# One pool of three PSUM banks for transposes, column sums and probabilities in a hybrid decoder layer

## The chip, the core and the metric

The kernel runs on one core of a Trainium2 chip. The time is device microseconds of one execution; a profiled execution gives the trace from which all rows below come. TensorE (PE) multiplies and transposes and writes its results into PSUM, which has eight banks of 128 x 512 float32 numbers; VectorE (DVE) and ScalarE (ACT) read the banks and work on the results. The engines have one queue of instructions each, and they meet by semaphores.

## What is computed

One layer of a decoder trunk over 512 tokens, 1024 channels, in float32. The parts that matter here:

```
h = rms_norm(x, attn_norm) * (1.0 + scale_a) + shift_a
... = jnp.split(h @ w_in, IN_OFFSETS, axis=-1)
...
o_a = nsa_mixer(q_a, kc, vc, ks, heads(nvs, G), kw, heads(nvw, G), g_nsa)   # 8 heads, 3 branches
...
q_b = (rms_norm(cq, mla_cq_norm) @ w_uq).reshape(B, S, MLA_HEADS, MLA_QK_DIM)
kv_b = (rms_norm(ckv, mla_ckv_norm) @ w_ukv).reshape(...)
...
o_b = mla_mixer(q_b, k_b, v_b)                                              # 8 heads
x = x + gate_a * ((g_a * o_a + g_b * o_b) @ w_o)
...
x = x + gate_f * ((jax.nn.silu(gt) * val) @ w_down)                         # gated MLP with conv
```

Mixer A (NSA) has a compressed, a selected and a window branch per head; with 512 tokens the selected branch is causal attention over all keys, and so is the window branch. Mixer B (MLA) makes its queries, keys and values from two latents, `cq` and `ckv`. Each large product is done as three float32r products of high and low halves.

## The kernel before, in words

The program has four stages, which follow each other with some overlap: the input projections and the compressed keys and values (to about 145 us of the span), the attention of eight head pairs (about 145 to 530 us), the output projection with the second norm (to about 580 us), and the MLP (to the end).

In the attention stage the code of a round `h` stands in this order: `nsa_head(h)`, `mla_kv(h)`, for even `h` `mla_q_pair(h // 2)` (the queries of two MLA heads), `bgate(h)`, for `h = 3` `kv_group(1)`, `q_head(h + 1)`, `comb_a`, `bgate(8 + h)`, `mla_head(h)`, `comb_b`, and, for `h` below 6, a matrix-vector product on DVE with its column sums (`gemv_cols`) or its row (`gate_out`). Round 7 is written out by halves.

An attention head is done in two halves of the queries (`half`), an NSA head in two branches of two halves each, which makes four passes; I call them A and B (queries 0 to 255, the two branches), C and D (queries 256 to 511). A pass does the score matmuls into two banks `psS`, a minimum over the masked scores on DVE (L762), the exponentials on ACT (L767), a scaling by the reciprocal of the sum (L776 on ACT, L778 on DVE), the transposes of the probabilities `Pt` on PE into banks `psT` (L790), their split into high and low halves (`PTh` on ACT, `PTl` on DVE, helper `split`, L83 and L84), and the products with the values into `psO`. Pass C of an NSA head is followed by the compressed branch (`cmp_lane`, L799 to L819).

`mla_kv(h)` makes `kraw` (normed keys, in a buffer of the tag `qn` of which there is one) and transposes it (L406) and the rotary part `krp` (L410). `mla_q_pair` does four products per pair into banks `psG` (`cqTh`), copies them to `qn` (the same single buffer, once per half) and transposes those (L355, L363). `q_head` squares the queries and sums them by matmuls with ones.

The order of the instructions on each engine is not written by hand: a scheduler places them when the program is built, by the order of the code and priorities, and it takes a tile's buffer from its tag's pool when one comes free. In the built program the tiles of one tag get their buffers in the order in which the code asks for them (in the pools of PSUM with one exception before and two after). The banks are such pools: S, T, O, G, and F, with the numbers in `BANKS` (L68). T holds the transposed probabilities (and the transposes and sums of the first stage and of the second norm); F holds the latent transposes (`kraw`, `krp`, `qn`, `a`, `cqn`, `ckvn`, `kn`), the column sums (`sqT`, `acc`), the rows of `gate_out` and a few accumulators.

Of the kernel before, what the change touches and what calls it, by code (L numbers as in the profile page):

```python
# [17 lines left out]
P = 128  # L18
S = 512
# [8 lines left out]
NF = DFF // P  # L28
# [10 lines left out]
def tile_hybrid_layer(  # L39
# [27 lines left out]

    BANKS = {"S": 2, "T": 2, "O": 1, "G": 2, "F": 1}  # L68

    def bank(tag):  # L70
        return ps.tile([P, 512], F32, name="ps" + tag, tag=tag, bufs=BANKS[tag])

# [154 lines left out]
    def kv_group(g, s1=None, s2=None, tag="G"):  # L227
# [20 lines left out]
        def post_k(th, b):  # L248
            if not tabl:
                for src in (rope_c, rope_s):  # L250
                    rope_table(raw_unit(), src)
            s4 = sm.tile([P, 4], F32, name="s4")
            for i in range(4):
                sumsq(b[:, i * HD:(i + 1) * HD], s4[:, i:i + 1])
            r4 = sm.tile([P, 4], F32, name="r4")
            rstd(r4, s4, HD, [P, 4])
            gk = g_k.rearrange("p a d -> p (a d)")[:, None, :].to_broadcast([P, 2, 256])
            a = rope_2x2(b, th, gk, 2, "kg", tabl[0], tabl[1])
            kn = pj.tile([P, 512], F32, name="kn", tag="qg")
            vec.tensor_mul(kn.rearrange("p (a d) -> p a d", a=4), a.rearrange("p (a d) -> p a d", a=4),  # L260
                           r4.unsqueeze(2).to_broadcast([P, 4, HD]))
            tr = bank("F")
            for br in range(2):
                for tt in range(2):
                    pe.transpose(tr[:, (br * 2 + tt) * P:(br * 2 + tt + 1) * P],
                                 kn[:, (tt * 2 + br) * P:(tt * 2 + br + 1) * P], ident)
            for br in range(2):
                cs = slice(th * 256 + 32 * (1 - br), (th + 1) * 256 + 32 * (1 - br))
                split(Kt[br][0][:, cs], Kt[br][1][:, cs], tr[:, br * 256:(br + 1) * 256])
# [13 lines left out]
    def q_head(h):  # L283
        b = bank("G")
# [8 lines left out]
        act.activation(sq, b, AF.Square)  # L293
        sb = bank("F")
        for t in range(NT):
# [17 lines left out]
    def mla_q_pair(p):  # L313
# [6 lines left out]
        for th in range(2):  # L320
            qn = pj.tile([P, 2, 2, HD], F32, name="qn", tag="qn")
            qr = pj.tile([P, 2, 2, RD], F32, name="qr", tag="qr")
            for tt in range(2):
                t = 2 * th + tt
                ts = slice(t * P, (t + 1) * P)
                b = bank("G")
# [24 lines left out]
            cs = slice(th * 256, (th + 1) * 256)  # L351
            tr = bank("F")
            for h in range(2):
                for tt in range(2):
                    pe.transpose(tr[:, (h * 2 + tt) * P:(h * 2 + tt + 1) * P], qn[:, tt, h, :], ident)  # L355
            for h in range(2):
                tv = tr[:, h * 256:(h + 1) * 256]
                act.activation(qnh[h][:, cs], tv, AF.Copy, scale=gcol)
                vec.scalar_tensor_tensor(qnl[h][:, cs], tv, gcol, f(qnh[h][:, cs]), op0=ALU.mult, op1=ALU.subtract)
            tr = bank("F")  # L360
            for h in range(2):
# [12 lines left out]
    def mla_kv(h):  # L374
# [6 lines left out]
        for th in range(2):  # L381
            b = bank("G")
# [8 lines left out]
            for tt in range(2):  # L391
# [11 lines left out]
                          rk.unsqueeze(2).unsqueeze(3).to_broadcast([P, NT, 2, RD]), op=ALU.mult)  # L403
        tr = bank("F")
        for t in range(NT):
            pe.transpose(tr[:, t * P:(t + 1) * P], kraw[:, t, :], ident)  # L406
        split(knh, knl, tr)
        tr = bank("F")
        for t in range(NT):
# [6 lines left out]
    with tc.tile_pool(name="p1", bufs=1) as p1:  # L416
# [9 lines left out]
        tr = bank("T")  # L426
# [76 lines left out]
        bA = [bank("G"), bank("G"), bank("S"), bank("S")]  # L503
        bF = [bank("O"), bank("F"), None]
        wk = {}
# [31 lines left out]
        tr = bank("T")  # L537
# [8 lines left out]
        for t in range(NT):  # L546
            b = bA[t]
# [14 lines left out]
        bB = [bank("G"), bank("G"), bank("S"), bank("S")]  # L562
        bV1 = bank("F")
        W_PRIO[0] = 100
# [11 lines left out]
        for g in range(2):  # L576
            b = bF[g]
# [36 lines left out]
        for src, nk, dst, nm in ((cqn, 3, cqT, "cqT"), (ckvn, 2, ckvT, "ckvT")):  # L614
            for k in range(nk):
                tr = bank("F")
                for t in range(NT):
                    pe.transpose(tr[:, t * P:(t + 1) * P], src[t][:, k * P:(k + 1) * P], ident)
                hh, hl = slot("cq", f"{nm}h{k}", F32R), slot("cq", f"{nm}l{k}", F32R)
                split(hh, hl, tr)  # L620
                dst.append((hh, hl))
# [82 lines left out]
    def gate_out(row, acc, i):  # L704
        b = bank("F")
        ah, al = (pj.tile([P, 512], F32R, name=n, tag=g) for n, g in (("gh", "t1"), ("gl", "t2")))
        split(ah, al, acc)
        mm(b, onesr, ah, True, False)
        mm(b, onesr, al, False, True)
        act.activation(row[:, i * 512:(i + 1) * 512], b, AF.Copy, scale=0.5)  # L710
# [5 lines left out]
    with tc.tile_pool(name="p2", bufs=1) as p2:  # L716
# [141 lines left out]
        def gemv_cols(acc, c0, dst, plus1):  # L858
            bcols = bank("F")
            for i in range(4):  # L860
# [40 lines left out]
        vec.tensor_mul(fA, fA, colB[:, 0:8])  # L901
        Oa, Ob = bank("O"), bank("F")
        mla_kv(7)
# [11 lines left out]
    with tc.tile_pool(name="p3", bufs=1) as p3:  # L915
# [46 lines left out]
        for th in range(2):  # L962
            for nb in range(2):
                cs = slice(nb * 512, (nb + 1) * 512)
                bs = [bank(s) for s in (("G", "G"), ("S", "S"), ("G", "G"), ("O", "F"))[2 * th + nb]]
                for k in range(KD):
# [15 lines left out]
        def ff_load(i, tag=None):  # L982
            FF[i] = [(bank(("OF" if i == 2 else "GS")[hv]), [load_w([(w_up, (hv * NF + i) * P, P)], 4 * u, 4, None, tag) for u in range(2)])
                     for hv in range(2)]
# [45 lines left out]
        for nh in range(2):  # L1030
            bs = [bank(s) for s in (("O", "F", "T", "T") if nh == 0 else ("G", "G", "S", "S"))]
            for k0, kn in [(k, 1) for k in range(NF - 4 * nh)] + [(NF - 4, 4)] * nh:
# [91 lines left out]
```

## Time and profile before

| | |
|---|---|
| median of 3 runs | 933.03 us (933.02 to 934.61) |
| the profiled execution | 934.68 us |
| its span, first to last instruction | 932.5 us |
| PE busy | 900.3 us, 97% |
| DVE busy | 689.5 us, 74% |
| ACT busy | 510.2 us, 55% |
| DMA | 113 MB, 121 GB/s on average |

A busy share is a mean over the stages. Matmuls overlap in PE's pipeline, so that the mean duration of one is longer than the time from one start to the next.

### The profile page before, as it was taken

The page shows a single profiled execution, that of the slowest core. Times are in us where ns is not written, and L with a number is a line of the kernel's source. Part 1 is how long each engine was busy: PE and PEld are TensorE (multiplying, and loading weights), DVE is VectorE, ACT ScalarE, POOL GpSimd, SP SyncE. Part 2 cuts the span into 40 slices and gives each one's busy share as a digit, 9 for nine tenths or more (in the row PEclk, how much of TensorE's full clock was granted, in tenths as well). Part 3 has the DMA queues.
Part 4 walks back from the last instruction along what each step waited for, and adds up shares of the span by engine and source line. Part 5 has one row for each costly group of instructions (what it writes and reads, how often), then busy time and mean ns, then how long its engine had stood idle before and what let it go on. Part 6 is the DMA issues. An engine that isn't in the chain of part 4 may idle for free.

```text
span 932.5 us, 14798 instructions
## 1 busy us (share of the span) xinstructions
PE 900.3 (97%) x5079; PEld 791.5 (85%) x5079; DVE 689.5 (74%) x1505; ACT 510.2 (55%) x1241; POOL 50.9 (5%) x57
## 2 busy tenths in 40 slices
PE   4999999999999999999999999999999999999998
PEld 3899888889899998889898889888888888888886
DVE  7967979798977779789877798797786676622423
ACT  5546858566676657559766764554444444422220
POOL 1000111011000001001010010000000000000000
PEclk9999999999999999999999999999999999999999
DMA  9945672541331263341214253363453333232431
GB/s 296 346 120 162 191 209 77 148 134 40 116 90 35 58 175 108 95 139 35 67 49 151 98 182 113 93 190 93 121 168 94 97 95 102 91 102 92 145 91 46
DMA packets 131681, 113.05 MB, mean 121 GB/s; under 512 B 7514, under 2 KB 110486, under 8 KB 131606
## 3 DMA queue, kind: packets, MB, share of 16 engines
q1 hardware_dynamic: 130838, 110.00, 39.9%
q0 software_dynamic: 768, 2.11, 0.7%
q8 instruction: 40, 0.66, 0.3%
q14 instruction: 35, 0.29, 0.1%
HBM read 109.98 MB, written 2.10 MB: 120 GB/s over the span
## 4 chain that ended last, share of the span: by engine, by line
PE 87%; ACT 4%; DVE 4%; DMA 3%; issue 1%; SPq 0%; POOL 0%; DVEq 0%; ACTq 0%
PE psG L87 41%; PE psS L87 24%; PE psO L87 9%; PE psF L87 5%; PE psT L87 4%; PE psT L790 2%; DVE wl L84 1%; ACT wh L83 1%; ACT Pt L767 1%; DMA ada<-in_w_ada_dram 1%; DMA x<-in_x_dram 1%; DMA wr<-in_cmp_k_w_dram 1%; DMA wr<-in_w_in_dram 0%; DMA wr<-in_cmp_v_w_dram 0%; ACT sq L223 0%
## 5 line engine op out<-in xcount | busy, mean ns | idle before, releaser
L83 ACT ACTIVATE wh<-wr 128x512 fp32r<-128x512 f32 (+3 forms) x304 | 186.9, 622 | 290.0 <-PE psS L87 103.8
L84 DVE TENSOR_TENSOR wl<-wr,wh 128x512 fp32r<-128x512 f32 (+3 forms) x304 | 203.5, 675 | 158.1 <-ACT wh L83 151.3
L87 PE MATMUL psG<-hTh,wh 128*128 128x512 f32 x192 | 76.5, 399 | 1.0 <-DVE qr L335 1.0
L87 PE MATMUL psG<-hTl,wh 128*128 128x512 f32 x192 | 76.3, 397 | 0.0
L87 PE MATMUL psG<-hTh,wl 128*128 128x512 f32 x192 | 76.2, 397 | 0.0
L87 PE MATMUL psS<-h2l,wh 128*128 128x512 f32 (+1 forms) x184 | 68.2, 371 | 0.0
L87 PE MATMUL psG<-h2h,wl 128*128 128x512 f32 (+1 forms) x184 | 68.2, 371 | 0.0
L87 PE MATMUL psG<-h2l,wh 128*128 128x512 f32 (+1 forms) x184 | 68.1, 371 | 0.0
L87 PE MATMUL psG<-h2h,wh 128*128 128x512 f32 (+1 forms) x184 | 68.1, 372 | 0.0
L87 PE MATMUL psS<-h2h,wl 128*128 128x512 f32 (+1 forms) x184 | 68.0, 371 | 0.0
L87 PE MATMUL psS<-h2h,wh 128*128 128x512 f32 (+1 forms) x184 | 68.0, 371 | 0.0
L767 ACT ACTIVATE Pt<-psS,nm 128x128 f32<-128x128 f32 (+2 forms) x96 | 51.3, 535 | 26.5 <-DVE nm L762 18.9
L84 DVE TENSOR_TENSOR PTl<-psT,PTh 128x384 fp32r<-128x384 f32 (+1 forms) x72 | 42.1, 597 | 6.7 <-ACT PTh L83 6.1
L122 DVE SCALAR_TENSOR_TENSOR acc<-wr,csil,acc 128x512 f32<-128x512 f32 x60 | 44.8, 746 | 3.0 <-DMA wr<-in_w_ada_dram 1.8
L83 ACT ACTIVATE PTh<-psT 128x384 fp32r<-128x384 f32 (+1 forms) x72 | 36.6, 529 | 16.5 <-PE psT L790 16.2
L87 PEld LDWEIGHTS psG<-hTh,wh 128*128 128x128 f32 x192 | 36.2, 188 | 7.6 <-PE psS L87 0.7
L87 PEld LDWEIGHTS psG<-hTh,wl 128*128 128x128 f32 x192 | 36.2, 188 | 6.6
L87 PEld LDWEIGHTS psG<-hTl,wh 128*128 128x128 f32 x192 | 36.1, 188 | 6.4
L87 PEld LDWEIGHTS psG<-h2h,wl 128*128 128x128 f32 x184 | 34.7, 188 | 6.1
L87 PEld LDWEIGHTS psG<-h2h,wh 128*128 128x128 f32 x184 | 34.7, 188 | 6.0
L87 PEld LDWEIGHTS psS<-h2h,wh 128*128 128x128 f32 x184 | 34.7, 188 | 6.0
L87 PEld LDWEIGHTS psS<-h2l,wh 128*128 128x128 f32 x184 | 34.7, 189 | 5.9
(454 smaller groups left out, 2524.2 us busy)
## 6 DMA issues: line engine op xcount, KB each, us to landing
wr<-in_w_up_dram SPq DMA_DIRECT2D x88, 256.0 KB, 3.0
wr<-in_w_ada_dram SPq DMA_DIRECT2D x64, 256.0 KB, 2.8
wr<-in_w_in_dram SPq DMA_DIRECT2D x48, 256.0 KB, 3.0
wr<-in_w_down_dram SPq DMA_DIRECT2D x44, 256.0 KB, 2.6
ada<-in_w_ada_dram SPq DMA_DIRECT2D x32, 256.0 KB, 5.4
wr<-in_w_o_dram SPq DMA_DIRECT2D x32, 256.0 KB, 3.1
wr<-in_w_in_dram SPq DMA_DIRECT2D x32, 128.0 KB, 3.0
wr<-in_cmp_k_w_dram SPq DMA_DIRECT2D x16, 256.0 KB, 3.4
```

Of the source, the lines that this page charges most:

```text
L83: act.activation(hi, src, AF.Copy)
L84: vec.tensor_sub(lo, src, f(hi))
L87: ins = pe.matmul(o, lhsT, rhs, start=start, stop=stop, skip_group_check=True)
L122: vec.scalar_tensor_tensor(acc, w, csil[:, k:k + 1], acc, op0=ALU.mult, op1=ALU.add)
L767: act.activation(Pt[:, off[x2]:off[x2] + nt[x2]], Sb[x2], AF.Exp, bias=nm[:, x2:x2 + 1], scale=-1.0, accum_out=sums[:, x2:x2 + 1])
L790: pe.transpose(tr[:, e * P:(e + 1) * P], Pt[:, o:o + P], ident)
```

## The change

`F` is gone from the pools, and `T` has three banks in place of two; each call of `bank("F")` becomes `bank("T")`. The number of banks is eight as before, and no instruction that computes is added or removed.

```diff
-    BANKS = {"S": 2, "T": 2, "O": 1, "G": 2, "F": 1}
+    BANKS = {"S": 2, "T": 3, "O": 1, "G": 2}
...
@@ kv_group, mla_q_pair (twice), mla_kv (twice), the transposes of cqn and ckvn
-            tr = bank("F")
+            tr = bank("T")
...
@@ q_head
-        sb = bank("F")
+        sb = bank("T")
...
@@ first stage
-        bF = [bank("O"), bank("F"), None]
+        bF = [bank("O"), bank("T"), None]
...
-        bV1 = bank("F")
+        bV1 = bank("T")
...
@@ gate_out, gemv_cols, round 7
-        b = bank("F")
+        b = bank("T")
...
-            bcols = bank("F")
+            bcols = bank("T")
...
-        Oa, Ob = bank("O"), bank("F")
+        Oa, Ob = bank("O"), bank("T")
...
@@ output projection, MLP
-                bs = [bank(s) for s in (("G", "G"), ("S", "S"), ("G", "G"), ("O", "F"))[2 * th + nb]]
+                bs = [bank(s) for s in (("G", "G"), ("S", "S"), ("G", "G"), ("O", "T"))[2 * th + nb]]
...
-            FF[i] = [(bank(("OF" if i == 2 else "GS")[hv]), ...
+            FF[i] = [(bank(("OT" if i == 2 else "GS")[hv]), ...
...
-            bs = [bank(s) for s in (("O", "F", "T", "T") if nh == 0 else ("G", "G", "S", "S"))]
+            bs = [bank(s) for s in (("O", "T", "T", "T") if nh == 0 else ("G", "G", "S", "S"))]
```

The scheduler orders the instructions anew. The places below are in round 0; rounds 2, 4 and 6 have the same pattern.

PE before, from pass B of NSA head 0 on: scores of pass B (`Kh_1067`, the window keys), the transposes of `kraw` and `krp`, the first scores of pass C, and two of the four products of the MLA query pair (`cqTh`, `cqTl`).

```order
L87 MATMUL psS<-Kh_1067,ql 128x256
L406 MATMUL psF<-ident,kraw 128x128 x4
L87 MATMUL psS<-Kh_1065,qh 128x416
L87 MATMUL psS<-Kl_1066,qh 128x416
L87 MATMUL psS<-Kh_1065,ql 128x416
L410 MATMUL psF<-ident,krp 128x128 x4
L87 MATMUL psG<-wh,cqTh_1016 128x384
L87 MATMUL psG<-wl,cqTh_1016 128x384
```

Before, the transposes of `kraw` and `krp` stand ahead of the first transpose of probabilities of this head.

PE after the change, the end of the same head: the products of pass C with the values, the transposes of pass D, one product of the compressed branch, and the transposes of `kraw`.

```order
L87 MATMUL psO<-PTh,Vh_1741 128x256
L790 MATMUL psT<-ident,Pt 128x128 x4
L87 MATMUL psO<-PTl,Vh_1741 128x256
L87 MATMUL psO<-PTh,Vl_1742 128x256
L87 MATMUL psO<-PTh,Vh_1741 128x128
L87 MATMUL psO<-PTl,Vh_1741 128x128
L87 MATMUL psO<-PTh,Vl_1742 128x128
L790 MATMUL psT<-ident,Pt 128x128 x3
L87 MATMUL psO<-pt,vc_107 128x512
L406 MATMUL psT<-ident,kraw 128x128 x4
```

After the change `kraw` is transposed behind all the transposes of the head's probabilities, and from the head's first scores to that row there is no product into `psG` on PE.

DVE after the change, where the same head begins (`kraw`, `krp` are the normed keys that PE is to transpose; `sc`, `psS` and `nm` belong to pass A).

```order
L401 TENSOR_TENSOR kraw<-kraw,rk 128x512
L84 TENSOR_TENSOR ql<-a_1849,qh 128x512
L402 TENSOR_TENSOR krp<-krr,rk 128x512
L760 TENSOR_TENSOR sc<-psS,tabs 128x32 x2
L762 ISA psS,nm<-psS,maskr,nrq 128x128
L762 ISA nm 128x1
L762 ISA psS,nm<-psS,maskr,nrq 128x256
```

`kraw` and `krp` are made on DVE ahead of the head's first minimum (before, behind the minima of pass A); 39 further rows of DVE follow that all belong to this head, up to its last `PTl`, and then come `knl` and the work of the query pair. Before, `kraw`, `knl`, weight splits and the query pair's work stand between these rows.

## Rows read from the trace of the kernel before

**Rows 1.** Windows: busy time of PE, PEld, DVE, ACT, POOL; clock, DMA share, GB/s.

```profile
140.00:560.00 420.00, 412.61 (x2606) 372.19 (x2605) 349.27 (x900) 282.42 (x815) 36.71 (x35) 1.00 0.35 100
146.90:184.20 37.30, 35.30 (x207) 31.16 (x207) 31.12 (x85) 25.88 (x76) 2.64 (x2) 1.00 0.42 121
...
560.00:928.00 368.00, 367.14 (x1731) 308.45 (x1729) 229.22 (x356) 143.66 (x242) 1.64 (x3) 1.00 0.36 108
```

**Rows 2.** Waits of PE from 140 to 560 us: total, times, longest.

```profile
PE psS L87 <- ACT Pt L767: 3.2, 4, 1.2
PE psG L87 <- DVE qr L335: 1.0, 2, 0.5
```

**Rows 3.** Chain that ended last, in order of time, round 0: start, us, what.

```profile
147.06 0.73 PE psS L87 x6
...
149.36 0.73 PE psS L87 x6
150.09 0.45 PE psF L406 x4
...
151.56 0.83 PE psS L87 x3
...
154.40 0.70 PE psS L87 x3
155.09 1.39 PE psG L87 x8
...
158.18 0.70 PE psS L87 x3
...
166.93 0.52 PE psO L87 x5
...
169.12 0.77 PE psT L790 x7
```

**Rows 4.** DVE groups by form, 140 to 560 us: count, busy us, mean ns, idle before.

```profile
L84 DVE TENSOR_TENSOR PTl<-psT,PTh 128x384 fp32r<-128x384 f32 x48 | 26.5, 551 | 5.1 <-ACT PTh L83 4.9
L84 DVE TENSOR_TENSOR PTl<-psT,PTh 128x512 fp32r<-128x512 f32 x24 | 16.5, 688 | 1.6 <-ACT PTh L83 1.2
L762 DVE DVE_READ_ACCUMULATOR2_ANT nm<- 128x1 f32 x96 | 13.4, 139 | 0.1
L762 DVE CUSTOM_DVE_ANT_0 psS<-psS,maskr,nrq 128x512 f32<-128x512 f32 x16 | 12.0, 752 | 2.1 <-PE psS L87 1.9
L762 DVE CUSTOM_DVE_ANT_0 psS<-psS,maskr,nrq 128x384 f32<-128x384 f32 x16 | 9.9, 621 | 0.9 <-PE psS L87 0.8
L762 DVE CUSTOM_DVE_ANT_0 psS<-psS,maskr,nrq 128x256 f32<-128x256 f32 x16 | 7.8, 487 | 0.8 <-PE psS L87 0.8
L770 DVE RECIPROCAL r<-sums 128x2 f32<-128x2 f32 x48 | 7.8, 162 | 6.4 <-ACT Pt L767 5.9
L778 DVE TENSOR_SCALAR Pt<-Pt,r 128x512 f32<-128x512 f32 x16 | 7.7, 481 | 0.2
...
L762 DVE CUSTOM_DVE_ANT_0 psS<-psS,maskr,nrq 128x128 f32<-128x128 f32 x16 | 5.6, 351 | 1.5 <-PE psS L87 1.4
L778 DVE TENSOR_SCALAR Pt<-Pt,r 128x256 f32<-128x256 f32 x16 | 5.6, 348 | 0.1
```

**Rows 5.** ACT groups by form, 140 to 560 us, same columns.

```profile
L767 ACT ACTIVATION_READ_ACCUMULATOR Pt<-psS,nm 128x1 f32 x96 | 20.1, 209 | 0.0
L767 ACT ACTIVATE Pt<-psS,nm 128x512 f32<-128x512 f32 x24 | 16.7, 698 | 9.6 <-DVE nm L762 5.3 <-DVE ms L132 3.7 <-DVE nrq L308 0.3
L776 ACT ACTIVATE Pt<-Pt,r 128x384 f32<-128x384 f32 x24 | 15.2, 632 | 0.7 <-DVE r L770 0.7
L83 ACT ACTIVATE PTh<-psT 128x512 fp32r<-128x512 f32 x24 | 14.4, 599 | 2.7 <-PE psT L790 2.7
L767 ACT ACTIVATE Pt<-psS,nm 128x384 f32<-128x384 f32 x24 | 14.0, 582 | 0.9 <-DVE sc L760 0.7 <-DVE nm L762 0.2
L805 ACT ACTIVATE pc<-sc,nbc,rq 128x32 f32<-128x32 f32 x32 | 12.9, 419 | 0.8 <-DVE nbc L801 0.8
```

**Rows 6.** Timeline of PE: start, us, what, idle before and its releaser.

```profile
29.42 0.61 PE L87 MATMUL psT<-onesr,acc 128*128 128x1 f32 x4 [0.32 <-DVE bp L486]
...
71.13 0.50 PE L87 MATMUL psF<-hTh,wh 128*128 128x512 f32 x1 [0.35 <-DVE a L582]
...
111.71 0.39 PE L87 MATMUL psO<-wh,X 128*128 128x256 f32 x1 [1.92 <-ACT hs L651]
```

**Rows 7.** Windows behind that last wait, columns as in rows 1.

```profile
112.50:116.00 3.50, 3.50 (x22) 3.50 (x21) 3.50 (x9) 2.79 (x9) 0.94 (x1) 0.64 0.41 131
116.00:120.00 4.00, 4.00 (x32) 4.00 (x31) 2.17 (x5) 1.12 (x2) 2.58 (x1) 0.89 0.91 269
```

More of the change, by code (lines that the diff above doesn't have):

```diff
@@ L351, in mla_q_pair @@
             cs = slice(th * 256, (th + 1) * 256)
-            tr = bank("F")
+            tr = bank("T")
             for h in range(2):
@@ L359, in mla_q_pair @@
                 vec.scalar_tensor_tensor(qnl[h][:, cs], tv, gcol, f(qnh[h][:, cs]), op0=ALU.mult, op1=ALU.subtract)
-            tr = bank("F")
+            tr = bank("T")
             for h in range(2):
@@ L403, in mla_kv @@
                           rk.unsqueeze(2).unsqueeze(3).to_broadcast([P, NT, 2, RD]), op=ALU.mult)
-        tr = bank("F")
+        tr = bank("T")
         for t in range(NT):
@@ L407, in mla_kv @@
         split(knh, knl, tr)
-        tr = bank("F")
+        tr = bank("T")
         for t in range(NT):
@@ L615, in tile_hybrid_layer @@
             for k in range(nk):
-                tr = bank("F")
+                tr = bank("T")
                 for t in range(NT):
@@ L982, in ff_load @@
         def ff_load(i, tag=None):
-            FF[i] = [(bank(("OF" if i == 2 else "GS")[hv]), [load_w([(w_up, (hv * NF + i) * P, P)], 4 * u, 4, None, tag) for u in range(2)])
+            FF[i] = [(bank(("OT" if i == 2 else "GS")[hv]), [load_w([(w_up, (hv * NF + i) * P, P)], 4 * u, 4, None, tag) for u in range(2)])
                      for hv in range(2)]
```

## The prediction, made before the changed kernel ran

> **What bounds the kernel now.** I read the windows first. From 560 us to 928 us PE is busy 367.1 of 368 us, and in the attention stage, from 140 to 560 us, 412.6 of 420 us [rows 1]. The reader is to see that PE sets the pace nearly everywhere, and that what a better order could win in the attention is at most the 7.4 us in which PE idles there. DVE is close behind in the same stage: 349.3 of 420 us. Then the waits of PE: the largest kind, 3.2 us in four waits, is scores for which a bank `psS` comes free only when the exponentials have read it; a second, 1.0 us, is the query pair [rows 2]. No wait of PE there is for a bank of T or F. Last the chain of round 0: while the passes of head 0 wait for DVE and ACT, PE runs other work, the transposes of `kraw` (0.45 us) and products of the query pair (0.17 us each, from 1.39 us for eight) [rows 3]. That cover is the point of the case.
>
> **What the change moves.** It adds and removes no work. What it alters is who stands behind whom. The buffers of a tag are handed out in the order of the code. Before, T and F were two such lines, and the work of the latents (F) could run ahead of the head whose probabilities stood in T. With one line, `kraw` of round `h` gets a bank only behind the last probabilities of NSA head `h`, since `nsa_head(h)` stands ahead of `mla_kv(h)` in the code. The order of the changed program shows it, and it shows what else then stands still: `kraw` holds the single buffer `qn`, so `mla_q_pair` cannot copy its products out of `psG`; both banks G stay full, and `bgate`, `q_head` and the rest of the pair, which all need G, wait. In rounds 0, 2, 4 and 6 PE thus has the NSA head almost alone, and DVE and ACT have nothing else in their queues either (on DVE 43 rows in a line of this head only). In odd rounds there is no query pair, G is emptied without `qn`, and `bgate` and `q_head` still cover the head.
>
> **The price of a head alone, from rows.** PE's own work, counted over the order's rows from the first scores to the transposes of `kraw`: scores 0.73 for pass A, 0.73 for B, 0.83 + 0.70 for C, 0.70 + 0.70 for D and some 0.2 for three narrow ones; 24 transposes at 0.11 us (0.77 for seven); 24 products with the values at 0.10 us (0.52 for five) and one of the compressed branch, some 0.2 [rows 3]. Together 9.9 us.
>
> The chain through the four passes, which share two banks `psS`: A to B 2.3 us and B to C 2.2 us, read from the starts 147.06, 149.36 and 151.56, where before the waits already ended with the exponentials [rows 3]. C to D: scores 1.5, two minima with their readings 0.62 + 0.75 + 2 x 0.14, two exponentials with theirs 0.70 + 0.58 + 2 x 0.21: 4.9 us [rows 3 to 5]. From D's first scores to its last transposes ACT decides: its queue has the four exponentials of the compressed branch first (4 x 0.63), then an exponential of D (0.79), the scaling of C (0.63), the other exponential (0.91), two copies of C's split (1.1, each at most 0.60), the scaling of D (0.63), and PE the transposes (0.77): 7.3 us [rows 3, 5]. To `kraw`, behind the compressed product, another 1 us or so. In sum 17.7 us for 9.9 us of PE work: PE stands still for 7.8 us. The lower bound is DVE with no gap at all: eight minima 4.42, eight readings 1.11, four scalings 1.66, six `PTl` 3.58, sixteen small ones of about the reciprocal's 0.16 or a little more, 2.8, and two of the compressed branch that I price like a `PTl`, 1.2: 14.8 us [rows 4]. Less 0.6 for readings that overlap and 1.2 for the two `PTl` behind the last transposes, and with 0.9 us until the first scores are there, 13.9 us, a stall of 4.0.
>
> Heads 2, 4 and 6 overlap with the end of the MLA head before them. The order's rows, priced alike, give PE 13.6, 16.0 and 13.2 us (head 4 has two products of the pair among them), DVE 17.6, 21.0 and 16.4. I lay half of DVE's extra over 14.8 on the chain of 17.7, and for head 4 take 21.5, since DVE's own sum is more: stalls of 5.5, 5.5 and 5.3 us. By DVE alone, with the same corrections, they would be 3.1, 4.1 and 2.3.
>
> In heads 1 and 5 the filler runs out ahead of the last pass: 4.2 and 3.4 us of PE rows stand between D's scores and its last transposes, for which the chain above wants 7.3 - 2.5 = 4.8 us even where the compressed exponentials are done by then. That is 0.6 and 1.4 us short, and where they are not done, up to 2.5 us more; I take 1.5 us each, 3 us. The lower bound is nothing.
>
> Against it stand gains. I let all 7.4 us of PE's idle time between 140 and 560 us go, since the new stalls replace them. In the first stage two waits of 0.3 us, one for the sums in T and one for bank F until the keys are out of it, need not remain [rows 6]: 0.7 us. After 560 us the order of PE is the same from the third MLP block on but for one small row, and PE idles 0.9 us there in all [rows 1].
>
> The sum: 7.8 + 5.5 + 5.5 + 5.3 + 3.0 - 7.4 - 0.7 = +19.0 us. The profiled execution of before took 934.7 us and the median is 933.0, so I predict 952.0 us for the median (953.7 for an execution like the profiled one).
>
> One rule speaks against this sum. The Trainium skill, page "Perfetto Trace Analysis", section "Matmuls", wants independent matmul groups to rotate through different banks, so that the evacuation of one overlaps the matmuls of the next; by it three banks for the transposes would be a gain. The trace does not bear it out here: no wait of PE in the stage is for a bank of T.
>
> **The rivals.**
> *The lone heads are packed (slower, but little).* DVE's queue could run without gaps, as it nearly does in round 0 now: 31.1 of 37.3 us busy [rows 1]. Then only DVE's sums count: 4.0 + 3.1 + 4.1 + 2.3 - 8.1 = +5.4, or 938.4 us. Against it: pass C cannot begin before B's exponentials whatever DVE does.
> *The stalls slow PE's clock as well.* Behind the one wait of 1.9 us before, the granted clock fell: 0.64 and 0.89 of full in the next two windows, a stretch of them at the lower level of 1.2 GHz [rows 6, 7], that is 1.26 + 0.44 = 1.7 us lost if PE would have been the bound. Lone heads have gaps as long. Each of four would add up to 1.7 us: 952.0 + 6.8 = 958.8; with a longer chain (half a us more in each of the 12 steps between passes) 964.8. For it: the gaps; against it: while PE waits anyway a slower clock costs only the scores and transposes on the chain. The Trainium skill, page "TensorE: Matmul & The Clock Gate", section "HAM oscillation", describes the same: a clock halved after each wait, paid again each time.
> *The wider pool pays (faster).* If transposes were held by banks, three of them would free PE earlier: the 7.4 + 0.7 us would go and no stall come, 924.9 us. It decides if PE idles for T. But no such wait is in the list [rows 2], and the order has the head alone.
> *No change.* The chain's waits would have to be hidden by work that the order does not show; the gains would cancel the stalls only if these came to 8.1 us in all, below DVE's own bound: 933.0 us.
>
> **How the numbers follow.** A measurement tells 0.2%, 1.9 us, from no change. Chances: the forecast (944 to 959 us) 0.60; packed heads (935 to 944) 0.18; clock or longer chains (959 to 972) 0.14; no change 0.04; faster 0.04. So slower 0.92, same 0.04, faster 0.04. The range from 940 to 965 leaves out 0.04 + 0.04, about half of the packed case's 0.18, which is spread upwards from 938, and a few hundredths above.
>
> **What would show it.** In the changed profile: PE idle before `psT` of line 790 and before `psS`, released by ACT `Pt` and DVE, bunched in four stretches of about 18 to 22 us; in each the transposes of `kraw` come behind all of line 790; PE's idle time in the attention stage 7.4 + 19.7 = about 27 us in place of 7.4; busy sums of DVE and ACT unchanged; from the MLP on the same rows, shifted. I would be wrong if PE were kept busy in those stretches by work whose place in the order I misread, if the last `PTl` of head 0 came within 14 us of its first scores, or if new waits in the first stage (T now holds three long accumulators there) cost more than they save.

## The result, and the profile after

The changed kernel takes 957.0 us (median, 955.7 to 959.1) against 933.6 for the kernel before: a ratio of 1.0254, 95% interval 1.0242 to 1.0266. The predicted time was 952.0 and the range 940 to 965. The profiled execution took 956.64 us, with a span of 954.9.

The page's first part, busy time by engine:

```profile
PE 909.2 (95%) x5079; PEld 794.3 (83%) x5079; DVE 696.5 (73%) x1505; ACT 512.2 (54%) x1241; POOL 49.5 (5%) x57
```

Of the 22.4 us by which the span grew, PE idles 13.5 (45.7 for 32.2) and is busy 8.9 longer for the same instructions, which stand further apart or run at a lower clock. ACT's sum is nearly unchanged, DVE's is 1% more.

Windows of the changed kernel (PE, PEld, DVE, ACT, POOL, clock, DMA share, GB/s): the attention; from the first scores to `kraw` in heads 0, 2, 4 and 6; last, two places, each with the stretch ahead of it, in which the clock fell.

```profile
140.00:560.00 420.00, 399.49 (x2496) 356.81 (x2497) 336.26 (x862) 269.69 (x784) 33.64 (x32) 0.99 0.32 90
149.50:167.50 18.00, 13.63 (x76) 11.54 (x77) 13.59 (x45) 10.66 (x35) 0.47 (x1) 0.81 0.01 1
244.60:262.70 18.10, 15.20 (x109) 13.43 (x110) 14.40 (x49) 13.48 (x41) 0.00 (x0) 1.00 0.01 1
358.40:377.20 18.80, 16.97 (x123) 15.72 (x123) 16.75 (x56) 15.41 (x55) 1.71 (x2) 1.00 0.07 16
454.30:471.40 17.10, 14.76 (x103) 12.96 (x104) 14.71 (x49) 13.40 (x42) 0.00 (x0) 1.00 0.01 1
...
138.00:150.80 12.80, 8.31 (x55) 7.17 (x53) 5.98 (x19) 7.07 (x29) 3.04 (x3) 1.00 0.13 35
150.80:157.60 6.80, 5.08 (x17) 4.37 (x18) 5.00 (x21) 3.18 (x11) 0.00 (x0) 0.50 0.00 1
570.00:577.40 7.40, 5.06 (x30) 4.01 (x29) 7.03 (x16) 2.61 (x7) 0.00 (x0) 1.00 0.32 97
577.50:580.90 3.40, 3.40 (x10) 2.63 (x9) 2.88 (x6) 2.46 (x5) 0.00 (x0) 0.50 0.20 57
```

Against [rows 1] PE's idle time in the attention is 20.5 us for 7.4. The four lone heads are there: 17 to 19 us each, DMA nearly at rest, DVE and ACT both with gaps, so that neither alone sets the length. The granted clock stands at its lower level in two places, 6.8 us in head 0 and 3.4 us at 577.5 (and for about 1 us at the very end); before there was one such place [rows 7].

Waits of PE in the attention, to be laid beside [rows 2]:

```profile
PE psS L87 <- ACT Pt L767: 4.2, 8, 1.2
PE psO L87 <- DVE PTl L84: 3.5, 10, 0.5
PE psT L815 <- DVE p L811: 3.3, 3, 1.3
PE psT L790 <- ACT Pt L776: 3.1, 3, 1.6
PE psS L87 <- ACT qh L83: 2.5, 1, 2.5
PE psG L87 <- DVE vl L84: 1.2, 1, 1.2
```

The first four are waits for the steps of a head; none of the six is for a free bank of T (the first row is, as before, a bank `psS` that the exponentials have yet to read). The two that stand last are new in kind: they lie ahead of head 0. PE's timeline shows them (the last bracket of a row is the idle time before it):

```profile
28.17 0.50 PE L87 MATMUL psT<-onesr,acc 128*128 128x1 f32 x4
...
61.26 0.39 PE L87 MATMUL psT<-hTh,wh 128*128 128x512 f32 x1
...
149.58 0.34 PE L87 MATMUL psS<-Kh,qh 128*128 128x160 f32 x1 [2.50 <-ACT qh L83]
...
153.34 0.47 PE L87 MATMUL psS<-Kh,qh 128*128 128x128 f32 x1 [1.16 <-ACT Pt L767]
...
155.29 0.69 PE L87 MATMUL psS<-Kh,qh 128*128 128x416 f32 x1
...
156.48 0.63 PE L87 MATMUL psS<-Kh,qh 128*128 128x512 f32 x1
156.91 0.63 PE L87 MATMUL psS<-Kl,qh 128*128 128x512 f32 x1
...
159.78 0.44 PE L87 MATMUL psS<-Kh,qh 128*128 128x384 f32 x1 [0.41 <-ACT Pt L767]
...
161.21 0.39 PE L87 MATMUL psS<-Kl,qh 128*128 128x512 f32 x1
161.44 0.39 PE L87 MATMUL psS<-Kh,ql 128*128 128x512 f32 x1
...
167.03 0.52 PE L790 MATMUL psT<-ident,Pt 128*128 128x128 f32 x3
...
167.62 0.60 PE L406 MATMUL psT<-ident,kraw 128*128 128x128 f32 x4
...
244.64 0.34 PE L87 MATMUL psS<-Kh,qh 128*128 128x160 f32 x1 [0.61 <-ACT Pt L767]
...
262.83 0.38 PE L406 MATMUL psT<-ident,kraw 128*128 128x128 f32 x2
...
358.43 0.29 PE L87 MATMUL psS<-Kh,qh 128*128 128x160 f32 x1
...
377.33 0.38 PE L406 MATMUL psT<-ident,kraw 128*128 128x128 f32 x2
...
454.33 0.34 PE L87 MATMUL psS<-Kh,qh 128*128 128x160 f32 x1 [0.64 <-ACT Pt L767]
...
471.53 0.27 PE L406 MATMUL psT<-ident,kraw 128*128 128x128 f32 x1
...
520.44 0.39 PE L87 MATMUL psG<-wh,uh 128*128 128x512 f32 x1
...
576.43 0.47 PE L87 MATMUL psT<-wh,uh 128*128 128x512 f32 x1 [2.34 <-DVE hf L958]
```

Head 0 reads as the prediction's chain: A at 149.58, B at 153.34, C at 155.29, D at 159.78, its last transposes at 167.03, and `kraw` at 167.62, behind all of line 790. The wait of 2.34 us at 576.43 is the output projection's last accumulator, which now asks for a bank of T behind the transposes of the second norm.

Two rows that stand in every one of these kernels cut the span in three: the first scores of head 0 (`128x160`) and the first product of the output projection (`psG<-wh,uh`, in round 7). Before, in the same view:

```profile
146.90 0.23 PE L87 MATMUL psS<-Kh,qh 128*128 128x160 f32 x1
...
500.46 0.40 PE L87 MATMUL psG<-wh,uh 128*128 128x512 f32 x1
```

So the first stage took 146.9 us before and 149.6 after (+2.7), the attention 353.6 and 370.9 (+17.3), the rest 432.0 and 434.5 (+2.4). Between the cuts of the attention PE idles 16.3 us for 6.6 before; the other 7.6 us of the 17.3 are PE being busy longer.

The first cut does not stand at quite the same place in the work. Eighteen of the first query pair's products (`cqTh`, `cqTl`) stand ahead of it in the changed kernel, nine in the kernel before. Nine take 1.6 us, so that with the same work on both sides the first stage lost 1.1 us and the attention 18.9.

### The profile page after: what moved, and what is told of

Read it like the earlier page. It is cut to its first block, busy times and chain, and to the rows that moved or that the text cites. A ratio compares the mean times of both kernels' runs of the same rounds, so it can differ in the third digit from the quotient of the medians.

```text
span 954.9 us, 14822 instructions
## 1 busy us (share of the span) xinstructions
PE 909.2 (95%) x5079; PEld 794.3 (83%) x5079; DVE 696.5 (73%) x1505; ACT 512.2 (54%) x1241; POOL 49.5 (5%) x57
## 4 chain that ended last, share of the span: by engine, by line
PE 84%; DVE 7%; ACT 5%; issue 2%; POOL 1%; DMA 1%; SPq 0%; DVEq 0%; ACTq 0%
PE psG L87 39%; PE psS L87 23%; PE psT L87 9%; PE psO L87 8%; PE psT L790 2%; ACT Pt L767 1%; ACT pc L805 1%; DVE PTl L84 1%; DVE psS L762 1%; DVE wl L84 1%; ACT wh L83 1%; ACT PTh L83 1%; DMA x<-in_x_dram 0%; PE psT L460 0%; DMA wr<-in_w_in_dram 0%
## 5 line engine op out<-in xcount | busy, mean ns | idle before, releaser
L767 ACT ACTIVATE Pt<-psS,nm 128x128 f32<-128x128 f32 (+2 forms) x96 | 50.4, 527 | 35.4 <-DVE nm L762 29.5
L84 DVE TENSOR_TENSOR PTl<-psT,PTh 128x384 fp32r<-128x384 f32 (+1 forms) x72 | 41.8, 596 | 10.5 <-ACT PTh L83 10.2
L122 DVE SCALAR_TENSOR_TENSOR acc<-wr,csil,acc 128x512 f32<-128x512 f32 x60 | 44.8, 746 | 3.2 <-DMA wr<-in_w_ada_dram 2.3
L83 ACT ACTIVATE PTh<-psT 128x384 fp32r<-128x384 f32 (+1 forms) x72 | 36.1, 524 | 17.9 <-PE psT L790 11.9
L790 PE MATMUL psT<-ident,Pt 128*128 128x128 f32 x240 | 38.8, 279 | 3.1 <-ACT Pt L776 3.1
```

The costliest lines, as they stand in the source:

```text
L83: act.activation(hi, src, AF.Copy)
L84: vec.tensor_sub(lo, src, f(hi))
L122: vec.scalar_tensor_tensor(acc, w, csil[:, k:k + 1], acc, op0=ALU.mult, op1=ALU.add)
L767: act.activation(Pt[:, off[x2]:off[x2] + nt[x2]], Sb[x2], AF.Exp, bias=nm[:, x2:x2 + 1], scale=-1.0, accum_out=sums[:, x2:x2 + 1])
L790: pe.transpose(tr[:, e * P:(e + 1) * P], Pt[:, o:o + P], ident)
```

## The experiments

All times by these cuts, from each kernel's profiled execution; the medians are of the timed runs, the ratios against the kernel before on the same chip. The profiled execution can lie up to 2.3 us off the median, so the stages do not always add up to it. (The second cut can stand a little earlier or later in the work: in `order_tail_before` some 2 us earlier. Ahead of the first cut stand nine products of the pair, as before, in `latents_in_T`, in the three kernels that put the tail of the compressed keys and values (the compress tail) in S on top of the change, and in the two controls; in the others eighteen.)

| kernel | median us | ratio (95%) | first stage | attention | rest |
|---|---|---|---|---|---|
| before | 933.6 | 1 | 146.9 | 353.6 | 432.0 |
| changed | 957.0 | 1.0254 (1.0242 to 1.0266) | 149.6 | 370.9 | 434.5 |
| latents_in_T | 960.9 | 1.0296 (1.0272 to 1.0321) | 145.0 | 379.5 | 432.0 |
| sums_in_T | 945.4 | 1.0132 (1.0113 to 1.0150) | 147.6 | 365.3 | 432.5 |
| both_two_banks | 968.9 | 1.0376 (1.0361 to 1.0392) | 147.1 | 388.4 | 431.8 |
| kv_before_nsa | 939.4 | 1.0068 (1.0051 to 1.0085) | 150.1 | 353.2 | 433.4 |
| kv_only_ahead | 978.3 | 1.0475 (1.0452 to 1.0497) | 150.1 | 391.4 | 435.8 |
| kraw_own_tag | 992.9 | 1.0644 (1.0617 to 1.0670) | 151.9 | 406.1 | 434.1 |
| compress_tail_in_S | 947.0 | 1.0148 (1.0130 to 1.0166) | 141.4 | 368.7 | 432.9 |
| norm_in_S | 951.9 | 1.0198 (1.0182 to 1.0213) | 148.9 | 370.5 | 430.3 |
| tail_and_norm_in_S | 943.9 | 1.0105 (1.0092 to 1.0118) | 142.5 | 369.3 | 430.3 |
| all_mended | 930.2 | 0.9958 (0.9946 to 0.9970) | 142.5 | 353.5 | 431.7 |
| order_before | 940.7 | 1.0069 (1.0056 to 1.0081) | 148.2 | 358.0 | 432.2 |
| order_tail_before | 932.9 | 0.9993 (0.9983 to 1.0003) | 145.9 | 350.4 | 434.6 |

**One part alone: the latents.** On the kernel before:

```diff
@@ mla_q_pair (twice), mla_kv (twice)
-            tr = bank("F")
+            tr = bank("T")
```

> The kernel before with its T of two banks and F of one; only the transposes of kraw, krp, qn and a (mla_kv, mla_q_pair) ask for a bank of T. Order: kraw now stands 12.3 us of PE rows behind the first scores of head 0 and at most 2.6 us of products into psG stand in the 15 us behind them, so the lone heads are there; first stage, column sums and second norm keep the order of before. Main theory (the code order of one shared line makes the lone heads, these are the loss): 15 to 20 us slower than before, 948 to 954 us, with two stretches of PE idle time of 3 to 8 us in each even round. Rival 1 (the loss comes from the hand-over into the attention, the second norm and the clock drops that the other merged uses cause): within 3 us of before, 930 to 937 us. Rival 2 (both, in equal parts): about 945 us.

It cost 27.4 us, more than the 15 to 20 that the main theory expected. The profiled execution lost 25.9 us in the attention; the first stage gained 1.9 and the rest lost nothing. Head 0 has only nine products of the pair for cover:

```profile
144.97 0.23 PE L87 MATMUL psS<-Kh,qh 128*128 128x160 f32 x1
...
162.55 0.60 PE L406 MATMUL psT<-ident,kraw 128*128 128x128 f32 x4
```

From the first scores to `kraw` it takes 17.6 us, and heads 2, 4 and 6 take 19.8, 22.1 and 20.0. The lone heads come from this part, and it costs more alone, in a line of two banks, than the whole change does with three. Rival 1 is out.

**The other part alone: sums and rows.**

```diff
@@ q_head
-        sb = bank("F")
+        sb = bank("T")
@@ gate_out
-        b = bank("F")
+        b = bank("T")
@@ gemv_cols
-            bcols = bank("F")
+            bcols = bank("T")
```

> The kernel before with T of two banks and F of one; only the column sums of q_head and gemv_cols and the rows of gate_out ask for a bank of T; the latents keep F. Order: kraw stands 0.5 us of PE rows behind the first scores, and 8 us of products into psG follow in the next 15 us: the cover stays. Main theory: 933 to 938 us (a wait of 2 to 4 us may come where the attention begins, since q_head's sums now stand behind the compress tails). Rival (any use that is moved into T's line costs alike, because the line as such holds PE up): 940 us or more.

It cost 11.9 us, nearly all of it in the attention, so the main theory's expectation missed and the rival's held. The clock is not the main reason: two of the four executions had a mean granted clock of 1.00 and took 944.1 and 944.4 us; the other two, the profiled one among them, had 0.996 and took 946.4 and 947.5. No head is alone here. The waits of PE in the attention:

```profile
PE psS L87 <- ACT Pt L767: 4.8, 5, 1.3
PE psT L790 <- ACT Pt L776: 2.7, 5, 1.1
```

They are again waits for the steps of heads. In the built program the column sums of round 0 (`gemv_cols`) now stand behind the first scores of head 1 (205.91 and 191.64 us), where they stood ahead of them (192.16 and 198.20). Which of the sums does the harm was not tried apart, nor whether they do any in the line of three banks.

**Both, with two banks.** The two edits above together; F stays for its other uses.

> The kernel before with both groups moved into the line of T, the latents of mla_kv and mla_q_pair and the sums and rows, but T keeps its two banks; F keeps only its uses in the first stage, in kv_group, in round 7 and behind the attention, and stands empty through most of the attention. Against the changed kernel (957) it lacks the third bank in the attention. The latents alone cost 27.4 us, the sums alone 11.9. If the costs of the two add up: 973 us, and the third bank in the common line is then worth about 16 us of what the merging costs. If the lone heads hide what the sums cost: 958 to 965 us, and the third bank is worth 1 to 8. If banks never limit T (the main theory as the prediction had it, which counts the number of banks for nothing): 955 to 960 us.

The two parts cost 35.4 us together, 3.9 less than their sum: 968.9 us lies between the first two expectations, and that the number of banks counts for nothing (955 to 960) is out. The changed kernel, with a third bank in the same line (and the remaining uses of F moved there too), is 11.9 us faster than this: in the attention 17.5, less some 5 lost elsewhere. Part of the 17.5 may be the clock's: this kernel has 20.5 us at the lower level in the attention, the changed kernel 6.8, which is up to 6.9 us. Here the rule that the prediction weighed (the Trainium skill, "Perfetto Trace Analysis", section "Matmuls": independent groups should rotate through different banks) has its place: a third bank is worth 11.9 us once everything stands in one line, though that is less than the line costs.

**Undoing the lone heads.** On the changed kernel, the code's order alone:

```diff
         for h in range(7):
-            Oa = nsa_head(h)
             mla_kv(h)
             if h % 2 == 0:
                 mla_q_pair(h // 2)
+            Oa = nsa_head(h)
```

> The changed kernel, with mla_kv(h) and, for even h, mla_q_pair called ahead of nsa_head(h) in the loop over rounds, so that kraw and qn ask for their banks of the shared T before the head's probabilities do. Order: kraw 0.5 us of PE rows behind the first scores, 8.6 to 10.4 us of products into psG in the next 15 us. Main theory: the stalls of the lone heads go (23 us of the 23.4), and what remains is what else the change cost, some 4 us at the hand-over and 4 us at the second norm, less what it gained: 933 to 942 us. Rival (three banks in one line, or the clock drops, cost by themselves): 950 us or more.

It took back 17.6 us, as the main theory expected, and by the cuts 17.7 in the attention, which is as long as before but for the nine products ahead of it (1.6 us). The timeline of head 0:

```profile
150.06 0.50 PE L87 MATMUL psS<-Kh,qh 128*128 128x160 f32 x1 [2.49 <-ACT qh L83]
...
151.33 1.09 PE L406 MATMUL psT<-ident,kraw 128*128 128x128 f32 x4
...
153.52 1.06 PE L355 MATMUL psT<-ident,qn 128*128 128x128 f32 x4
154.71 0.69 PE L87 MATMUL psG<-wh,cqTh 128*128 128x384 f32 x1
```

`kraw` and `qn` have their banks at once and the pair's products flow. The wait of 2.5 us ahead of the head stays, and so does the fall of the clock: 10 us between 142 and 156 us are at the lower level, so that this stretch is no part of what came back.

**Only half of that.** `mla_kv(h)` alone ahead of `nsa_head(h)`:

```diff
-            Oa = nsa_head(h)
             mla_kv(h)
+            Oa = nsa_head(h)
```

> The changed kernel, with only mla_kv(h) called ahead of nsa_head(h); mla_q_pair stays behind it. kraw then has its bank at once (0.5 us of PE rows behind the first scores) and gives up the buffer qn, so that the pair's first two products run (3.1 us of PE rows under heads 0 and 4), but the transposes of qn still stand behind the head's probabilities, and then psG is full again. Main theory with the clamp kraw, qn, psG: the lone heads get about 3 us of cover each in rounds 0 and 4 and lose kraw's wait in all rounds: 943 to 951 us, between the changed kernel and the 939.4 with both moved. Rival 1 (only kraw's place counts, qn's not): 937 to 942. Rival 2 (kraw's place doesn't count, the pair's does): 955 to 959.

It is 21.3 us slower than the changed kernel: all three expectations missed. Windows from the first scores to past the compressed product in heads 0, 2, 4 and 6, and a stretch in the first:

```profile
150.10:178.40 28.30, 21.49 (x101) 18.87 (x102) 22.21 (x65) 15.19 (x49) 2.05 (x2) 0.74 0.34 103
250.80:277.10 26.30, 22.27 (x137) 19.98 (x136) 24.45 (x71) 17.59 (x54) 1.63 (x1) 0.83 0.29 91
372.50:398.00 25.50, 20.98 (x128) 18.72 (x127) 23.98 (x71) 16.15 (x56) 3.35 (x3) 0.93 0.34 103
469.90:496.80 26.90, 23.00 (x130) 20.64 (x130) 21.65 (x66) 20.32 (x61) 1.86 (x1) 0.81 0.11 30
...
148.50:158.70 10.20, 7.61 (x26) 6.89 (x27) 7.51 (x23) 4.20 (x13) 2.02 (x2) 0.50 0.00 1
```

The heads are still nearly alone, and 7 to 11 us longer to the same place: DVE has 22 to 24 us of work in each, where the changed kernel's heads have 14 to 17, while PE gains only some 3 us of products (eighteen more). In head 0 the keys and the first half of the queries are 3.4 us of DVE's extra work; more of it, 5.7 us, is the matrix-vector product (`acc`, L120 and L122), and 2.0 us are splits of weights, which stood outside the changed kernel's head. Heads 2 and 4 are alike; in head 6 other splits stand in place of the matrix-vector product. And the clock falls in them: the mean granted clock is 0.976, which is 2 x 0.024 x 977 = 47 us at the lower level (1.2 GHz). The changed kernel has 11 us there, so that up to half of the difference, 18 of the 21.3 us, can be the clock's. The clock rival, wrong for the changed kernel's heads 2, 4 and 6, is right for this one. Behind these products no other into `psG` runs until the head's end, as the clamp (`qn` and `psG`) has it, but what the clock and the longer queue cost apart was not measured.

**The buffer of `kraw`.**

```diff
-        kraw = pj.tile([P, NT, HD], F32, name="kraw", tag="qn")
+        kraw = pj.tile([P, NT, HD], F32, name="kraw", tag="kr")
```

> The changed kernel, with kraw in a buffer of the tag kr in place of qn, so that mla_q_pair can fill qn and empty psG for its first half without waiting for kraw's transposes. Order: 3.1 us of products of the pair stand under head 0 and 3.8 us under head 2 (0 to 2 before this edit). Main theory with the single buffer qn as the clamp: 3 to 10 us faster than the changed kernel, 947 to 954 us; it can't give all back, since qn itself waits for a bank of T. Rival (the line of T alone holds everything, the buffer qn adds nothing): within 2 us of the changed kernel, 955 to 959 us.

35.9 us slower than the changed kernel, so both expectations missed: it freed `qn` but put `kraw` into another single buffer, that of `comb_b` (L874) and of the compress tail (L655, L674, L680). Windows of head 1, where the kernel before has PE busy all of 35.7 us; then the largest wait of PE in the attention:

```profile
201.90:231.00 29.10, 26.17 (x151) 21.77 (x151) 23.98 (x71) 18.34 (x53) 1.01 (x1) 1.00 0.36 102
```

```profile
PE psS L87 <- ACT Pt L767: 9.9, 18, 1.8
```

Odd rounds lose their cover as well. The mean granted clock is 0.975, some 50 us at the lower level for the changed kernel's 11, so that up to 19 of the 35.9 us can be the clock's. So it does not tell whether `qn` alone is the clamp; it fits that a single buffer which waits in T's line passes the wait on to all who share it, but the edit changed two things at once. That `qn` is the clamp is thus not shown by itself; it rests on the order and on the pair of kernels above.

**The hand-over into the attention.** On the changed kernel (L652, L659, L677):

```diff
-            ht = bank("T")
+            ht = bank("S")
...
-            o = bank("T")
+            o = bank("S")
...
-            tr = bank("T")
+            tr = bank("S")
```

> The changed kernel, with the tail of the compressed keys and values of the first stage (ht, o and the transposes of kcn) in banks S in place of T, so that the queries of head 0 no longer stand in one line with it. Lone heads as in the changed kernel. The changed kernel idles 1.2 us at 141.7, 2.5 us at 149.6 and 1.0 us at 151.4 there. If these waits are the line's: 3 to 5 us faster than the changed kernel, 952 to 954 us. Rival (they are the time that ACT and DVE take for the queries, whatever bank these stand in): within 1.5 us of it, 955.5 to 958.5.

10.0 us faster, twice what was expected. The first scores, a product of the pair and `kraw` in the timeline, and the windows ahead of head 0 and in it:

```profile
141.43 0.34 PE L87 MATMUL psS<-Kh,qh 128*128 128x160 f32 x1 [0.25 <-DVE tot L398]
...
142.56 0.44 PE L87 MATMUL psG<-wh,cqTh 128*128 128x384 f32 x1
...
157.62 0.60 PE L406 MATMUL psT<-ident,kraw 128*128 128x128 f32 x4
```

```profile
130.00:141.40 11.40, 11.18 (x71) 9.73 (x69) 7.23 (x18) 6.16 (x22) 1.38 (x1) 1.00 0.50 131
141.40:157.40 16.00, 13.52 (x85) 11.12 (x85) 13.30 (x47) 12.07 (x44) 1.01 (x1) 1.00 0.07 18
```

The wait for `qh` is gone, and the granted clock stays at 1.00 through the head, though PE has gaps there too. So the stretch at the lower level went with the idle time ahead of the head (PE busy 8.31 of 12.80 us there in the changed kernel). The head is not quite the same, though: nine products of the pair (1.6 us) now stand under its pass A, where the changed kernel has them ahead of the first cut.

The profiled execution is 12.0 us faster than that of the changed kernel: 8.2 in the first stage, 2.2 in the attention and 1.6 in the rest. With the nine products on the same side that is 6.6 in the first stage and 3.8 in the attention. The first stage is 5.5 us shorter than that of the kernel before, with the same nine products ahead of its end: the edit also wins time that the kernel before lost. Head 0 itself takes 16.2 us (141.43 to 157.62) for 18.0. The clock (at most 3.4 us, half of 6.8) and the wait for `ql` (1.0 us) are both gone there; what each cost was not measured apart.

**The second norm.**

```diff
-                bs = [bank(s) for s in (("G", "G"), ("S", "S"), ("G", "G"), ("O", "T"))[2 * th + nb]]
+                bs = [bank(s) for s in (("G", "G"), ("S", "S"), ("G", "G"), ("S", "S"))[2 * th + nb]]
```

> The changed kernel, with the last quarter of the output projection in two banks S in place of O and T, so that its accumulator no longer stands in one line with the transposes of the second norm. The changed kernel idles 2.34 us at 576.4 for it, and a stretch of half clock of 3.41 us follows. If the wait and the clock's fall belong together: 3.5 to 4.5 us faster, 952.5 to 953.5 us. If the wait goes and the clock falls all the same: 2 to 3 us faster, 954 to 955. If the wait only moves (S is busy there too): within 1 us of 957.

5.0 us faster, a little more than expected, 4.2 of them behind the second cut, and the granted clock is 1.00 there: wait and clock went together. The wait (2.3 us) and the clock (at most 1.7, half of 3.4) come to 4.0 of it.

**The two edits together, and all three.**

> The changed kernel with both edits whose effect was measured one by one: the compress tail in banks S (10.0 us faster) and the last quarter of the output projection in S (5.0). What is left of the change is the lone heads at the full clock and the other uses of the common line. If the two add up: 942 us, so that the lone heads, less all gains, cost 8.5 us against before. If they share something (the clock's fall behind either): 944 to 948. If the lone heads pay all of the loss, as the prediction had it: 950 or more.

13.1 us of 15.0 add up. What is left against before is 10.2 us, with 15.7 in the attention at full clock.

> The changed kernel with three banks in one line and its three couplings taken out: mla_kv and mla_q_pair ahead of nsa_head, the compress tail in S, the last quarter of the output projection in S. If what each gave alone (17.5, 10.0 and 5.0 us) adds up: 924.5 us, below before. Main theory (lone heads, hand-over and norm are three separate stalls, but the clock stretch of round 0 is counted in two of them): 926 to 931 us. Rival (a common line of three banks costs by itself, wherever its users stand): 936 or more.

930.2 us, 0.4% faster than before, as the main theory expected, and short of the sum by 5.7 us. The order of the code takes 13.7 us here. The attention is as long as before (353.5 us); what is won lies in the first stage. Its windows, of the attention and of head 0 with its cover:

```profile
140.00:560.00 420.00, 413.25 (x2595) 371.69 (x2594) 349.15 (x900) 283.62 (x808) 34.77 (x35) 1.00 0.35 101
...
142.40:180.20 37.80, 37.53 (x222) 33.04 (x223) 33.68 (x92) 27.90 (x88) 2.64 (x2) 1.00 0.45 126
```

**The controls on the kernel before:** the same order of the code, without and with the compress tail in S.

> A control: the kernel before, with T of two banks and F of one, and only mla_kv and mla_q_pair called ahead of nsa_head. In it the latents' line is F anyway, so that by the main theory their place in the code tells little: 931 to 936 us. Rival (the order of the code is worth something by itself, and what it gave the changed kernel was not the end of the lone heads): 925 us or less.

7.0 us slower than before: neither expectation held, but the rival, that the order gains by itself, is out. What the order gave the changed kernel was the end of the lone heads. Why the same order costs 7.0 us where the pools are separate was not looked into.

> The second control: the kernel before with its T of two and F of one, the same order of the code, and the compress tail in S. Beside the version with one line of three banks, which has the same two edits, it tells what the merging is worth when its couplings are out. Main theory (no wait of before was for a bank of T or F, so that a third bank gives little): both within 3 us of each other, here 929 to 934 us. Rival (the third bank pays once nothing stands in its way): the version with three banks is over 4 us faster than this one.

No difference from before: the main theory's expectation held. The version with one line of three banks is 2.8 us faster (930.2 against 932.9, 0.3%) with the same two edits; it has a third besides, the last quarter of the output projection in S, which this one lacks. By the cuts the difference lies in the first stage (142.5 for 145.9), where that third edit has no part, and not in the attention, so it fits a small gain of the merged pools once the couplings are out; a pair that differs in the pools alone was not run.

## Why the prediction was right, and where not

- **Code order, one line, lone heads:** shown. `kraw` comes behind all of line 790 in the four even rounds, the stall follows the latents alone (`latents_in_T`) and goes when they are asked for first (`kv_before_nsa`). The sizes are less sure: `sums_in_T` and `order_before`, which make no lone head, cost 11.9 and 7.0 us, so that a new order of the instructions alone can be worth that much.
- **The attention's net loss**, predicted 27.1 - 7.4 = 19.7 us: measured 17.3 by the cuts, 18.9 with the nine products counted alike. PE's idle time grew less than that, by 9.7 us between the cuts; in the window of the prediction's sign it is 20.5 us where about 27 were forecast, since PE's rows also stretched.
- **Head 0's chain**, 17.7 us: 18.04 by the rows (149.58 to 167.62), so a stall of 8.1 for 7.8. Its parts differ: A to B 3.8 for 2.3 (the late `ql` and half clock), B to C 2.0 for 2.2, C to D 4.5 for 4.9, D to the end of its last transposes 7.8 for 7.3, and `kraw` comes right behind them, where I had another 1 us. That the sum agrees is partly luck: with the clock at full (`compress_tail_in_S`) the same head takes 16.2 us, so that the chain of 17.7 was too dear by 1.5.
- **Heads 2, 4 and 6:** 18.2, 18.9 and 17.2 us, where I had 19.1, 21.5 and 18.5. With my sums of PE's work the stalls are 4.6, 2.9 and 4.0 for 5.5, 5.5 and 5.3. The term that was mis-sized is the chain of 17.7 that all three start from: against the 16.2 us of head 0 at the full clock they are 2.0, 2.7 and 1.0 longer, close to what I laid on them for DVE's extra work from the MLA head's end (1.4, 3.8 and 0.8).
- **The stalls' sum:** 8.1 + 4.6 + 2.9 + 4.0 = 19.6 us. It counts from my prices of PE's work; PE's idle time in the four windows is 4.4, 2.9, 1.8 and 2.3 us. In heads 1 and 5 PE idles 0.9 us (198.9 to 233.4) and 1.1 us (408.7 to 443.0), for 1.5 each. Together 21.6 for 27.1. The gain set against them, 7.4, can't be measured apart: what is left to the attention's loss is 21.6 - 17.3 = 4.3 us, or 2.7 with the nine products, and it holds whatever the column sums in T's line and the third bank did.
- **DVE as the bound** (the packed heads): wrong. DVE idles 4.4, 3.7, 2.1 and 2.4 us in the windows of the four heads.
- **The first stage**, -0.7: +2.7 by the cut, +1.1 without the nine products. The prediction named this as a sign that it would be wrong, new waits that cost more than they save, and it came true. Both waits that I let go are gone (no idle before 28.17 and 61.26), and more was lost at the end: `psG` behind `vl` and the first scores behind `qh`, with the queries' sums behind the compress tail. I had looked for new waits at the three long accumulators, and they lie in another place.
- **The rest of the program**, 0: +2.4. I read that the order is the same from the third MLP block on, and passed over the accumulator of the output projection, which stands ahead of that.
- **The clock**, a rival: half right. It fell, but behind the hand-over and behind the norm, not in the lone heads 2, 4 and 6; 10.2 us at the lower level (1.2 GHz) for 3.4 before, by [rows 7] (2 x 0.36 x 3.5 + 2 x 0.11 x 4.0), which is (10.2 - 3.4) / 2 = 3.4 us if PE was the bound throughout.

So the sum of 19.0 was 4.4 below the 23.4 of the medians: lone heads too dear, and hand-over, norm and clock left out. These errors have opposite signs, and that they partly cancel is luck. So is a second pair. The prediction counted the number of banks for nothing and put the place of the column sums at nothing; with two banks in the line its sum would have been much the same 19.0 us, and 35.4 us were measured (`both_two_banks`), while the sums alone cost 11.9 (`sums_in_T`). The mechanism is shown; the size came out near partly because the third bank gave back 11.9.

## What to carry to other kernels

Two pools of buffers are also two queues. Before they are merged, look in the built order for who then stands behind whom, above all for the work that covers a latency chain and for single buffers that its producers hold; call that work first. Against separate pools, merging gained here only with those couplings out, and little (2.8 us). Half of the mending can cost more than none (`kv_only_ahead`, 21.3 us), and the same order of the code cost 7.0 us where the pools were separate.

## What the runs showed of the hardware

The granted clock fell from 1.00 to 0.50 (the lower level) behind stretches in which PE was busy 8.31 of 12.80 us and 5.06 of 7.40 us, and stayed at 1.00 through heads in which it was busy 13.52 of 16.00 (`compress_tail_in_S`) and 15.20 of 18.10 us (head 2 of the changed kernel). It also fell in `latents_in_T` and `sums_in_T`, for two stretches of 3.4 us each in the attention, and in `both_two_banks` for 20.5 us there; what led up to these was not followed. At the lower level (1.2 GHz) the 128x512 scores of pass C start 0.43 us apart (156.48 and 156.91 in the timeline above), those of pass D, at the full clock, 0.23 (161.21 and 161.44).

With the waits at the hand-over and the norm taken away, the clock stayed full, and the two edits gained 10.0 and 5.0 us where the waits themselves are 4.7 and 2.3. The clock can account for at most 3.4 and 1.7 us of that, half of the time at the lower level; the rest is not explained. The Trainium skill, "TensorE: Matmul & The Clock Gate", section "HAM oscillation", tells of a clock that is halved after each wait and paid for each time; here it was so for these two waits, and in `kv_only_ahead` in every lone head, but not for the shorter gaps in the changed kernel's heads 2, 4 and 6.
